# New labels and a new priority table for the scheduler of a two-layer encoder

## The chip, the cores and the metric

The kernel runs on one core of one Trainium2 chip. Its time is device microseconds (us), the median of several runs. One further execution was recorded by the profiler; its durations are used for all steps below. Engines are named as in the profile: PE is TensorE's matmul, PEld its weight load, DVE is VectorE, ACT is ScalarE, POOL is GpSimd, SP issues most of the DMAs.

## The reference

The program is an encoder of two layers on one sequence of 256 tokens with 1024 channels, in float32:

```
def reference(x, ...):
    for l in range(DEPTH):                      # DEPTH = 2
        h = hybrid_mixer(x, ...)                # three mixers on x, gated merge, w_out
        x = layer_norm(DEEPNORM_ALPHA * x + h, ln1_g[l], ln1_b[l])
        f = conv_glu_ffn(x, ffn_up[l], ffn_conv[l], ffn_conv_b[l], ffn_down[l])
        x = layer_norm(DEEPNORM_ALPHA * x + f, ln2_g[l], ln2_b[l])
    return x

def conv_glu_ffn(x, w_up, conv_w, conv_b, w_down):
    gate, up = jnp.split(x @ w_up, 2, axis=-1)  # 2 x 2816 columns
    gate = dwconv_centred(gate, conv_w) + conv_b
    return (jax.nn.silu(gate) * up) @ w_down
```

The three mixers are a differential attention, a gated DeltaNet in chunks (forward and backward, each with a triangular solve and a scan), and a windowed attention. The sum of their gated outputs goes through `w_out`.

## The kernel before

All of it runs as one stream of recorded operations on one core. Every weight matrix is cut into pieces of 128 x 1024 numbers. A piece is loaded by a DMA on SP into a `raw` tile (4 buffers), copied by ScalarE or VectorE into a `hi` tile with fewer mantissa bits, and VectorE subtracts the two to give `lo`. Each matrix product is then three products (hi x hi, lo x hi, hi x lo). There are 4 `hi` and 4 `lo` tiles; they are given out in the order in which the program asks for weights, not in the order in which TensorE uses them. In the trace the pieces are called `raw_take`, `hi_take` and `lo_take`, or `hi_proj_tok` and `lo_proj_tok` for the output projections.

The program of a layer is: three mixers in threads that ask for projections (tiles `mm_proj_ch`, `mm_token_major`), the gate and branch products of the merge (`mm_product`), the output projection `wo` with the first norm (`proj_tok`, tiles `mm_run` and `ch_run`), the feed-forward stage, and the down projection `fd` with the second norm, by the same `proj_tok`. The DeltaNet's parts show as `decay` (POOL selects and ScalarE scalings that build `D_decay` and `N_decay`), `gdn`, `solve` and `scan`.

The feed-forward stage has 22 gate and 22 up tiles of 128 columns, in 11 chunks of two (`c` = 0 to 10, the loop from line 1471). A gate or up tile is a `wide` product, `mm_wide`: eight pairs of one matmul of 512 columns with `hi` and one of 256 with `lo`. For the chunks 0 and 1 the up half comes from one product with the tokens in rows (`token_major("ft", ...)`), whose result is then transposed by TensorE; in the trace these are the eight matmuls `tile_encoder_trunk<-tri,s_token_major` (layer 1: `ile_encoder_trunk<-tri,s_token_major`). Up times activated gate gives the two operands `h_` and `l_` of a chunk on VectorE and ScalarE, also named `tile_encoder_trunk`. The down projection reads chunk 0 first.

The order of all this isn't that of the program. A class `Plan` records each operation with its engine, a modelled cost and its dependencies (`record`, whose line 195 is therefore the line of every operation in the trace). `emit` gives each operation a rank: the modelled length of the longest path that starts from it, plus the operation's urgency, plus a number from the table `PRIO` that is looked up by the operation's label:

```
op.rank += op.urgent + PRIO.get(op.label, 0.0)
```

`schedule` then simulates the engines and the tile slots, and whenever an engine is free it takes, of the operations that can start first, the one of the highest rank. The operations are issued in the order of the simulated starts. On the chip each engine works through its own list in that order, and an instruction that has to wait holds up all that stand behind it on its engine. So the table `PRIO` (numbers in us) sets the order without touching what is computed. Before, only the parts of the mixers and of the merge have labels; `proj_tok`, the norms' ends and the feed-forward stage run with label `None` and priority 0.

Of the kernel before, what the change touches and what calls it, by code (L numbers as in the profile page):

```python
# [45 lines left out]
SPOT = {('ft', 0, 0): 'g', ('ft', 0, 1): 'g', ('ft', 0, 2): 'yc', ('ft', 1, 0): 'g', ('ft', 1, 1): 'g', ('ft', 1, 2): 'yc', ('av', 1, 0): 'h16'}  # L46
DIRECT = False
WHOLE = ()
PRIO = {(0, 'a', 'ak', 0): 2.2, (0, 'a', 'ak', 1): -4.9, (0, 'a', 'aq', 1): -2.6, (0, 'a', 0): 4.1, (0, 'a', 1): -5.5, (0, 'a', 2): 1.0, (0, 'a', 3): -2.7, (0, 'ab', 0): 4.3, (0, 'ak', 0): -2.5, (0, 'aq', 0): 1.1, (0, 'aq', 1): 1.1, (0, 'av', 0): 5.7, (0, 'c', 'ckv', 0): -8.6, (0, 'c', 'cq', 0): 1.8, (0, 'c', 'cq', 1): 9.5, (0, 'c', 0): -2.0, (0, 'c', 1): -1.0, (0, 'c', 2): -4.2, (0, 'c', 3): 4.2, (0, 'ckv', 0): -4.2, (0, 'cq', 0): 1.8, (0, 'cq', 1): 11.9, (0, 'finish'): 8.4, (0, 'gate', 0): -15.6, (0, 'gate', 1): -3.2, (0, 'gz', 1): -1.6, (0, 'gz', 3): 2.0, (0, 'gz', 4): -8.6, (0, 'gz', 5): -0.8, (0, 'k', 'gate', 0): 2.5, (0, 'k', 'k', 0): -7.3, (0, 'k', 'k', 1): -0.5, (0, 'k', 'q', 0): 1.6, (0, 'k', 'q', 1): -2.1, (0, 'k', 'v', 1): 0.3, (0, 'k', 0): -3.5, (0, 'k', 1): -5.6, (0, 'q', 1): 6.9, (0, 'scan'): -13.4, (0, 'v', 0): -0.8, (0, 'wb', 0): -7.9, (0, 'wb', 1): -20.3, (0, 'wb', 2): 9.2, (0, 'wb', 3): 0.9, (0, 'wb', 4): -5.6, (1, 'a', 'ak', 0): -4.0, (1, 'a', 'ak', 1): 6.5, (1, 'a', 'aq', 0): 5.4, (1, 'a', 'aq', 1): 3.6, (1, 'a', 3): 0.3, (1, 'ab', 0): -3.6, (1, 'ak', 0): 0.4, (1, 'ak', 1): 6.6, (1, 'aq', 1): -0.3, (1, 'c', 0): 6.5, (1, 'c', 1): 0.8, (1, 'c', 3): -10.4, (1, 'ckv', 0): -4.2, (1, 'cq', 0): 7.6, (1, 'cq', 1): -10.9, (1, 'finish'): 6.3, (1, 'gate', 0): 2.0, (1, 'gate', 1): -2.8, (1, 'gz', 0): -2.9, (1, 'gz', 2): 2.1, (1, 'gz', 3): -3.6, (1, 'gz', 4): 1.2, (1, 'gz', 5): 12.7, (1, 'k', 'ab', 0): -3.9, (1, 'k', 'gate', 0): 9.3, (1, 'k', 'gate', 1): 6.1, (1, 'k', 'k', 0): 4.3, (1, 'k', 'q', 0): -5.8, (1, 'k', 'q', 1): -4.7, (1, 'k', 'v', 0): 5.9, (1, 'k', 'v', 1): -1.4, (1, 'k', 1): -5.3, (1, 'q', 0): 10.2, (1, 'q', 1): -4.3, (1, 'scan'): -5.9, (1, 'solve'): -3.9, (1, 'wb', 0): -10.8, (1, 'wb', 1): -23.6, (1, 'wb', 3): 6.8, (1, 'wb', 4): 4.9, (1, 'wb', 5): 13.3, (0, 'k', 'ab', 0): -1.4, (0, 'k', 'gate', 1): -0.1, (0, 'k', 'v', 0): 4.3, (0, 'q', 0): 0.2, (1, 'aq', 0): -3.6, (1, 'av', 0): -1.9, (1, 'gz', 1): 0.7, (1, 'v', 0): 4.6, (1, 'wb', 2): 4.1}
LOADS = (11, 12, 12)  # L50
PIECES = 2
PAIRS = ("s", "yc")
# [86 lines left out]
class Plan:  # L139
# [99 lines left out]
    def emit(self):  # L239
# [45 lines left out]
        for op in ops:  # L285
            op.rank += op.urgent + PRIO.get(op.label, 0.0)
        self.schedule(users, order)
# [208 lines left out]
def tile_encoder_trunk(ctx: ExitStack, tc: tile.TileContext, a: dict, out: bass.AP, depth=DEPTH, tap=None):  # L496
    nc = tc.nc
    plan = Plan()
# [15 lines left out]
    def nm(base):  # L514
        import sys
        f = sys._getframe(2)
        base = f"{base}_{f.f_code.co_name}{f.f_lineno}"
        counts[base] = counts.get(base, 0) + 1
        return f"{base}_{counts[base]}"
# [4 lines left out]
    def buf(tag, shape=(P, 512), dtype=F32):  # L524
        return plan.tile(mp, shape, dtype, tag, nm(tag), BUFS[tag])
# [47 lines left out]
    x = cp.tile([P, 2, D], F32, name="x")  # L573
# [256 lines left out]
    def proj_tok(nme, l, nk, lhs, norm):  # L830

        nb = nk // 2
        order = [(half, b) for half in range(2) for b in range(nb)]
        plain, tags = KEEP[nme] if nme == "wo" else KEEP[nme][l]
        first = len(order) - plain - len(tags)
        ps = {}

        def run(half, b, w, tt, c0=0):
            n = 256 if half == tt == 1 and SPLIT else 512
            if (half, tt, c0) not in ps:  # L840
                ps[half, tt, c0] = (ps_ch if half == 1 and (c0 == 0 or SPLIT == 2) else ps_mm)((P, n))
            cs = slice(c0, c0 + n)
            for j in range(2):
                k = 2 * b + j
                lh, ll = lhs(k, tt)
                mm3(ps[half, tt, c0], lh, ll, w[0][j][:, cs], w[1][j][:, cs], k == 0, k == nk - 1)
            if b == nb - 1:
                u, plan.urgent = plan.urgent, HASTE if tt and half else HASTE0
                norm.part(tt, half * 512 + c0, n, ps[half, tt, c0])
                plan.urgent = u  # L850

        kept = []
        for n, (half, b) in enumerate(order):
# [679 lines left out]
```

## Time and profile before

| | us |
|---|---|
| median of 3 runs | 986.03 (985.98 to 986.37) |
| the profiled execution, its own time | 985.31 |
| its span in the trace | 983.6 |
| PE busy | 961.5 (98%) |
| PEld busy | 829.6 (84%) |
| DVE busy | 759.4 (77%) |
| ACT busy | 605.8 (62%) |
| POOL busy | 75.1 (8%) |

Busy time is the share of the span in which an engine executes at least one instruction. Matmuls overlap in the pipeline, so a matmul's shown length is longer than the step from one to the next. The trace also gives, for each instruction that its engine had to wait for, how long the engine was idle ahead of it and which instruction released it.

### The profile page before, as it was taken

How to read it: one execution, taken by the hardware profiler on the slowest of the kernel's cores; microseconds unless marked ns; L12 is line 12 of the kernel's file. 1: busy time of each engine (PE TensorE's matmuls, PEld its weight loads, DVE VectorE, ACT ScalarE, POOL GpSimd, SP SyncE). 2: the span in 40 equal slices, each digit the busy share in tenths (PEclk: the TensorE clock that was granted, in tenths of full speed). 3: DMA queues.
4: the chain of work that ended last, by engine and by line, in shares of the span. 5: the costliest groups of instructions: out<-in, count | busy, mean ns of one | idle time of the engine just before them, and what ended most of it. 6: DMA issues, size and time to landing. Idle time of an engine off the chain costs nothing.

```text
span 983.6 us, 16368 instructions
## 1 busy us (share of the span) xinstructions
PE 961.5 (98%) x6126; PEld 829.6 (84%) x6126; DVE 759.4 (77%) x1404; ACT 605.8 (62%) x1134; POOL 75.1 (8%) x84
## 2 busy tenths in 40 slices
PE   7999999999999999999999999999999999999996
PEld 6889899878888888878889998998778778888885
DVE  6799797666599988875689989866565988888655
ACT  5778757774465766653558777756744646666441
POOL 0510020000000100000005200100000010000000
PEclk9999999999999999999999999999999999999999
DMA  7554435355685766656635444334556665666661
GB/s 266 151 170 133 126 135 187 92 157 164 192 268 164 211 193 191 192 153 192 213 92 168 159 144 131 117 107 131 174 167 200 220 193 185 179 189 191 192 192 43
DMA packets 50100, 165.27 MB, mean 168 GB/s; under 512 B 5751, under 2 KB 11271, under 8 KB 50020
## 3 DMA queue, kind: packets, MB, share of 16 engines
q1 hardware_dynamic: 48644, 159.78, 52.3%
q0 software_dynamic: 1376, 4.43, 1.5%
q8 instruction: 48, 0.79, 0.3%
q14 instruction: 32, 0.26, 0.1%
HBM read 163.12 MB, written 1.07 MB: 167 GB/s over the span
## 4 chain that ended last, share of the span: by engine, by line
PE 83%; DVE 5%; ACT 4%; DMA 3%; issue 2%; POOL 2%; SPq 0%; POOLq 0%; ACTq 0%; DVEq 0%
PE mm_wide L195 23%; PE mm_product L195 19%; PE mm_proj_ch L195 15%; PE mm_run L195 7%; PE ch_run L195 6%; PE mm_token_major L195 3%; PE at_window L195 3%; PE ch_solve L195 2%; PE at_attention L195 2%; DMA raw_take<-in_w_dram 1%; ACT hi_take L195 1%; PE ch_gdn L195 1%; PE ch_finish L195 1%; PE ch_scan L195 1%; DVE lo_take L195 1%
## 5 line engine op out<-in xcount | busy, mean ns | idle before, releaser
L195 DVE TENSOR_TENSOR lo_take<-raw_take,hi_take 128x1024 fp32r<-128x1024 f32 x219 | 269.5, 1236 | 96.1 <-ACT hi_take L195 93.3
L195 ACT ACTIVATE hi_take<-raw_take 128x1024 fp32r<-128x1024 f32 x213 | 224.3, 1057 | 178.9 <-PE mm_wide L195 59.3
L195 PE MATMUL mm_wide<-xT,hi_take 128*128 128x512 f32 x640 | 224.0, 394 | 0.1
L195 PE MATMUL mm_proj_ch<-xT,hi_take 128*128 128x256 f32 x928 | 177.8, 287 | 1.1 <-ACT hi_take L195 1.1
L195 PE MATMUL mm_wide<-xT,lo_take 128*128 128x256 f32 x640 | 178.3, 283 | 0.0
L195 PEld LDWEIGHTS mm_proj_ch<-xT,hi_take 128*128 128x128 f32 x928 | 144.7, 189 | 4.2 <-ACT hi_take L195 1.7
L195 PEld LDWEIGHTS mm_wide<-xT,hi_take 128*128 128x128 f32 x640 | 119.4, 188 | 26.6 <-DVE xT L195 0.3
L195 PE MATMUL mm_proj_ch<-xT,lo_take 128*128 128x256 f32 x464 | 133.4, 288 | 0.0
L195 PE MATMUL mm_product<-hi_take,xT 128*128 128x512 f32 x384 | 128.4, 403 | 0.0
L195 PEld LDWEIGHTS mm_wide<-xT,lo_take 128*128 128x128 f32 x640 | 120.4, 188 | 1.4
L195 DVE TENSOR_TENSOR lo_proj_tok<-raw_proj_tok,hi_proj_tok 128x1024 fp32r<-128x1024 f32 x50 | 61.2, 1224 | 46.0 <-ACT hi_proj_tok L195 45.9
L195 ACT ACTIVATE hi_proj_tok<-raw_proj_tok 128x1024 fp32r<-128x1024 f32 x50 | 53.0, 1060 | 63.8 <-PE mm_run L195 35.0
L195 PEld LDWEIGHTS mm_proj_ch<-xT,lo_take 128*128 128x128 f32 x464 | 87.6, 189 | 2.7 <-DVE lo_take L195 1.1
L195 PEld LDWEIGHTS mm_product<-hi_take,xT 128*128 128x128 f32 x384 | 71.5, 189 | 15.4 <-issue 1.5
L195 PE MATMUL mm_product<-lo_take,xT 128*128 128x512 f32 x192 | 77.2, 402 | 0.0
L195 PEld LDWEIGHTS mm_product<-lo_take,xT 128*128 128x128 f32 x192 | 36.3, 189 | 6.8 <-DVE lo_take L195 0.2
L195 DVE SCALAR_TENSOR_TENSOR z_conv_silu<-mm_proj_ch,col_params,z_conv_silu 128x254 f32<-128x254 f32 (+1 forms) x96 | 39.4, 473 | 0.2
L195 POOL TENSOR_TENSOR s_tail<-s_tail,nhalf 128x1 f32<-128x1 f32 x8 | 8.2, 1023 | 383.4 <-DVE s_tail L195 383.4
L195 ACT ACTIVATE e_window<-e_window,s_window 128x256 f32<-128x256 f32 x54 | 25.7, 499 | 12.2 <-DVE s_window L195 12.1
L195 PEld LDWEIGHTS <-h_solve 128*128 128x128 f16 x640 | 25.6, 98 | 7.8 <-issue 3.4
L195 PE MATMUL mm_run<-hi_proj_tok,tile_encoder_trunk 128*128 128x512 f32 x88 | 27.5, 392 | 2.4 <-DVE tile_encoder_trunk L195 1.4
L195 PE MATMUL mm_run<-hi_proj_tok,ile_encoder_trunk 128*128 128x512 f32 x88 | 27.3, 390 | 0.0
(354 smaller groups left out, 1771.6 us busy)
## 6 DMA issues: line engine op xcount, KB each, us to landing
raw_take<-in_w_dram SPq DMA_DIRECT2D x226, 512.0 KB, 3.7
raw_proj_tok<-in_w_dram SPq DMA_DIRECT2D x60, 512.0 KB, 3.6
G_load_G<-band SPq DMA_DIRECT2D x24, 192.0 KB, 3.3
ya_ln_params<-in_lnp_dram POOLq DMA_DIRECT2D x16, 256.0 KB, 5.4
x<-in_xT_dram SPq DMA_DIRECT2D x4, 256.0 KB, 4.3
x<-in_x_dram SPq DMA_DIRECT2D x2, 512.0 KB, 4.5
out_dram<-x SPq DMA_DIRECT2D x8, 128.0 KB, 1.7
_tile_encoder_trunk<-in_w_dram SPq DMA_DIRECT2D x4, 128.0 KB, 5.1
```

What stands on the lines that cost most here:

```text
L195: op.ways.append((eng, lambda fn=fn, args=args, kw=kw: fn(*args, **kw), _cost(eng, name, outs, ins, args, kw), table))
```

## The change

The table `PRIO` is replaced: all its numbers are new, and it has entries for new labels. These labels are set in three places: in `proj_tok` for each weight piece (layer, `fd` or `wo`, half, piece), for the norm's two tails and for the pieces that are kept for a second pass; in the layer loop around the last step of a norm (`norms.pop().finish()`); and in the feed-forward stage for the token-major product and for each chunk. No operation, operand, tile or modelled cost is changed. Cut to its core:

```diff
-PRIO = {(0, 'a', 'ak', 0): 2.2, ...}
+PRIO = {(0, 'a', 'ak', 0): -4.7, ..., (0, 'f', 5): -8.9, ..., (0, 'ft'): 1.2, ..., (1, 'f', 7): -11.7, ...}
...
         kept = []
         for n, (half, b) in enumerate(order):
+            plan.label = (l, nme, half, b)
             w = weights((nme, l, half, b), tag=tags[n - first - plain] if n >= first + plain else None)
...
+        plan.label = (l, nme, "tail", 0)
         norm.tail(0)
+        plan.label = (l, nme, "kept")
         for c0 in (0, 256) if SPLIT else (0,):
...
+        plan.label = (l, nme, "tail", 1)
         norm.tail(1)
+        plan.label = None
...
         if norms:
+            plan.label = (l, "x", 2)
             norms.pop().finish()
+            plan.label = None
...
+        plan.label = (l, "ft")
         ft = token_major("ft", l, "s")
         for c in range(NFF // 2):
+            plan.label = (l, "f", c)
             pg = buf("h16", (P, 2, T))
...
             if c == 2:
+                plan.label = (l, "x", 1)
                 norms.pop().finish()
+        plan.label = None
         norm = Norm(l, 2, pr["ln2_g"], pr["ln2_b"], l == depth - 1)
```

How the order moves is seen in the engines' lists. In layer 0 ScalarE, where the DeltaNet's decay matrices are made, has this before (`N_decay` are the scalings that wait for POOL's selects, `hi_take_9` is the copy of the ninth weight piece):

```order
L195 ACTIVATE N_decay_1_125<-N_decay_1_125,nbeta_gdn_scalars_1_109 128x128 x4
L195 ACTIVATE N_decay_2_130<-N_decay_2_130,nbeta_gdn_scalars_1_109 128x128 x3
L195 ACTIVATE hi_take_9_182<-raw_take_9_181 128x1024
L195 ACTIVATE N_decay_2_130<-N_decay_2_130,nbeta_gdn_scalars_1_109 128x128
L195 ACTIVATE N_decay_3_135<-N_decay_3_135,nbeta_gdn_scalars_1_109 128x128 x4
L195 ACTIVATE N_decay_4_140<-N_decay_4_140,nbeta_gdn_scalars_1_109 128x128 x4
```

The ninth copy stands behind seven scalings. The same engine after, from four places ahead of the first copy of `D_decay`:

```order
L195 ACTIVATE hi_take_7_169<-raw_take_7_168 128x1024
L195 ACTIVATE q_token_major_1_154<-mm_token_major_1_153 128x512
L195 ACTIVATE hi_take_8_172<-raw_take_8_171 128x1024
L195 ACTIVATE hi_take_9_182<-raw_take_9_181 128x1024
L195 ACTIVATE D_decay_1_124<-ch_decay_1_123 128x512
```

and eleven places further on, where the scalings are:

```order
L195 ACTIVATE hi_take_10_185<-raw_take_10_184 128x1024
L195 ACTIVATE N_decay_1_125<-N_decay_1_125,nbeta_gdn_scalars_1_109 128x128 x4
L195 ACTIVATE N_decay_2_130<-N_decay_2_130,nbeta_gdn_scalars_1_109 128x128 x3
L195 ACTIVATE D_decay_4_139<-ch_decay_4_138 128x512
L195 ACTIVATE N_decay_2_130<-N_decay_2_130,nbeta_gdn_scalars_1_109 128x128
L195 ACTIVATE N_decay_3_135<-N_decay_3_135,nbeta_gdn_scalars_1_109 128x128 x4
L195 ACTIVATE hi_take_11_264<-raw_take_11_263 128x1024
```

The copies 7 to 10 have moved ahead of the scalings; the eleventh is now among them.

On TensorE, at the end of layer 0's feed-forward stage, before (`mm_wide_40` is the last up tile, `mm_run_3` the first tile of the down projection, which reads chunk 0; the transposes have `mm_` ahead of the trace's name, after their PSUM tile):

```order
L195 MATMUL mm_wide_40_969<-xT,hi_take_109_971 128x512
L195 MATMUL mm_wide_40_969<-xT,lo_take_109_972 128x256
L195 MATMUL mm_tile_encoder_trunk_1_770<-tri,s_token_major_1_757 128x128
L195 MATMUL mm_tile_encoder_trunk_1_770<-tri,s_token_major_2_759 128x128
L195 MATMUL mm_tile_encoder_trunk_1_770<-tri,s_token_major_1_757 128x128
L195 MATMUL mm_tile_encoder_trunk_1_770<-tri,s_token_major_2_759 128x128
L195 MATMUL mm_tile_encoder_trunk_2_783<-tri,s_token_major_1_757 128x128
L195 MATMUL mm_tile_encoder_trunk_2_783<-tri,s_token_major_2_759 128x128
L195 MATMUL mm_tile_encoder_trunk_2_783<-tri,s_token_major_1_757 128x128
L195 MATMUL mm_tile_encoder_trunk_2_783<-tri,s_token_major_2_759 128x128
L195 MATMUL mm_run_3_984<-hi_proj_tok_6_982,z_tile_encoder_trunk_1_771 128x512
L195 MATMUL mm_run_3_984<-lo_proj_tok_6_983,z_tile_encoder_trunk_1_771 128x512
```

After, the four transposes of chunk 0 stand some 400 rows earlier, between gate tiles (`mm_wide_12` and `mm_wide_17`), and those of chunk 1 earlier still:

```order
L195 MATMUL mm_wide_12_822<-xT,lo_take_81_825 128x256
L195 MATMUL mm_tile_encoder_trunk_1_770<-tri,s_token_major_1_757 128x128
L195 MATMUL mm_tile_encoder_trunk_1_770<-tri,s_token_major_2_759 128x128
L195 MATMUL mm_tile_encoder_trunk_1_770<-tri,s_token_major_1_757 128x128
L195 MATMUL mm_tile_encoder_trunk_1_770<-tri,s_token_major_2_759 128x128
L195 MATMUL mm_wide_17_850<-xT,hi_take_86_852 128x512
```

and the down projection's first matmul comes while chunk 5's up tiles (`mm_wide_19`, `mm_wide_20`) are unfinished:

```order
L195 MATMUL mm_wide_19_860<-xT,lo_take_88_863 128x256
L195 MATMUL mm_wide_20_864<-xT,hi_take_89_866 128x512
L195 MATMUL mm_wide_20_864<-xT,lo_take_89_867 128x256
L195 MATMUL mm_wide_20_864<-xT,hi_take_89_866 128x512
L195 MATMUL mm_wide_20_864<-xT,lo_take_89_867 128x256
L195 MATMUL mm_wide_20_864<-xT,hi_take_89_866 128x512
L195 MATMUL mm_wide_20_864<-xT,lo_take_89_867 128x256
L195 MATMUL mm_wide_20_864<-xT,hi_take_89_866 128x512
L195 MATMUL mm_wide_20_864<-xT,lo_take_89_867 128x256
L195 MATMUL mm_run_3_984<-hi_proj_tok_6_982,z_tile_encoder_trunk_1_771 128x512
```

The other matmuls of `mm_wide_19` stand 200 to 300 rows earlier; 18 other wide tiles (`mm_wide_21` to `mm_wide_38`) lie between. In layer 1 chunk 7's up tiles are treated alike, with 12 wide tiles between.

## Rows read from the trace of the kernel before

**Rows 1.** The page: busy time of each engine, its share of the span, instructions.

```profile
PE 961.5 (98%) x6126; PEld 829.6 (84%) x6126; DVE 759.4 (77%) x1404; ACT 605.8 (62%) x1134; POOL 75.1 (8%) x84
```

**Rows 2.** Timeline, TensorE's last matmuls: start, busy us, engine, line, operation.

```profile
973.68 0.84 PE L195 MATMUL ch_run<-g_weights,ile_encoder_trunk 128*128 128x512 f32 x3
```

**Rows 3.** Waits of TensorE, whole span: total us, times, longest us.

```profile
PE mm_proj_ch L195 <- ACT _tile_encoder_trunk L195: 5.9, 2, 4.9
PE mm_run L195 <- DVE tile_encoder_trunk L195: 1.4, 1, 1.4
PE mm_proj_ch L195 <- ACT hi_take L195: 1.1, 2, 0.8
PE mm_run L195 <- ACT tile_encoder_trunk L195: 1.0, 1, 1.0
PE ile_encoder_trunk L195 <- ACT s_token_major L195: 0.7, 1, 0.7
PE ch_solve L195 <- DVE h_solve L195: 0.7, 1, 0.7
PE mm_token_major L195 <- DVE xT L195: 0.6, 1, 0.6
PE ch_solve L195 <- ACT h_solve L195: 0.6, 2, 0.4
PE at_window L195 <- DVE s_window L195: 0.3, 1, 0.3
PE ch_gdn L195 <- ACT j_gdn L195: 0.3, 1, 0.3
PE at_window L195 <- DVE o_attention L195: 0.2, 1, 0.2
```

**Rows 4.** Timeline, end of layer 0's feed-forward stage; idle before and releaser in brackets.

```profile
428.20 0.39 PE L195 MATMUL mm_wide<-xT,hi_take 128*128 128x512 f32 x1
428.43 0.28 PE L195 MATMUL mm_wide<-xT,lo_take 128*128 128x256 f32 x1
...
428.55 0.40 PE L195 MATMUL mm_wide<-xT,hi_take 128*128 128x512 f32 x1
...
429.60 1.04 PE L195 MATMUL tile_encoder_trunk<-tri,s_token_major 128*128 128x128 f32 x8
...
431.64 0.50 PE L195 MATMUL mm_run<-hi_proj_tok,tile_encoder_trunk 128*128 128x512 f32 x1 [1.01 <-ACT tile_encoder_trunk L195]
...
432.31 3.08 DVE L195 TENSOR_TENSOR tile_encoder_trunk<-tile_encoder_trunk,tile_encoder_trunk 128x512 f32<-128x512 f32 x5
...
434.25 0.73 PE L195 MATMUL mm_run<-hi_proj_tok,tile_encoder_trunk 128*128 128x512 f32 x2 [1.41 <-DVE tile_encoder_trunk L195]
```

**Rows 5.** Timeline, layer 0's decay matrices, VectorE, POOL, ScalarE and TensorE.

```profile
34.61 3.22 DVE L195 TENSOR_TENSOR lo_take<-raw_take,hi_take 128x1024 fp32r<-128x1024 f32 x2
...
36.70 1.61 POOL L195 TENSOR_SCALAR_AFFINE_SELECT N_decay<-D_decay 128x512 f32<-128x512 f32 x1
...
38.35 2.16 ACT L195 ACTIVATE N_decay<-N_decay,nbeta_gdn_scalars 128x128 f32<-128x128 f32 x7 [2.33 <-POOL N_decay L195]
...
40.42 1.04 ACT L195 ACTIVATE hi_take<-raw_take 128x1024 fp32r<-128x1024 f32 x1
...
41.52 0.63 PE L195 MATMUL mm_proj_ch<-xT,hi_take 128*128 128x256 f32 x3 [0.80 <-ACT hi_take L195]
```

**Rows 6.** Timeline, the first solve of layer 0, and the transposes of layer 1.

```profile
72.07 0.62 PE L195 MATMUL ch_solve<-id,h_solve 128*128 128x128 f16 x8 [0.66 <-DVE h_solve L195]
...
806.51 0.60 ACT L195 ACTIVATE s_token_major<-mm_token_major 128x512 f32<-128x512 f32 x1 [0.42 <-PE mm_token_major L195]
...
807.16 0.33 PE L195 MATMUL ile_encoder_trunk<-tri,s_token_major 128*128 128x128 f32 x1 [0.69 <-ACT s_token_major L195]
```

**Rows 7.** Timeline, two weight slots of four in use, layer 0's feed-forward stage.

```profile
377.41 1.23 DVE L195 TENSOR_TENSOR lo_take<-raw_take,hi_take 128x1024 fp32r<-128x1024 f32 x1 [0.64 <-ACT hi_take L195]
...
379.51 0.28 PE L195 MATMUL mm_wide<-xT,lo_take 128*128 128x256 f32 x1
```

More of the change, by code (lines that the diff above doesn't have):

```diff
@@ L48 @@
 WHOLE = ()
-PRIO = {(0, 'a', 'ak', 0): 2.2, (0, 'a', 'ak', 1): -4.9, (0, 'a', 'aq', 1): -2.6, (0, 'a', 0): 4.1, (0, 'a', 1): -5.5, (0, 'a', 2): 1.0, (0, 'a', 3): -2.7, (0, 'ab', 0): 4.3, (0, 'ak', 0): -2.5, (0, 'aq', 0): 1.1, (0, 'aq', 1): 1.1, (0, 'av', 0): 5.7, (0, 'c', 'ckv', 0): -8.6, (0, 'c', 'cq', 0): 1.8, (0, 'c', 'cq', 1): 9.5, (0, 'c', 0): -2.0, (0, 'c', 1): -1.0, (0, 'c', 2): -4.2, (0, 'c', 3): 4.2, (0, 'ckv', 0): -4.2, (0, 'cq', 0): 1.8, (0, 'cq', 1): 11.9, (0, 'finish'): 8.4, (0, 'gate', 0): -15.6, (0, 'gate', 1): -3.2, (0, 'gz', 1): -1.6, (0, 'gz', 3): 2.0, (0, 'gz', 4): -8.6, (0, 'gz', 5): -0.8, (0, 'k', 'gate', 0): 2.5, (0, 'k', 'k', 0): -7.3, (0, 'k', 'k', 1): -0.5, (0, 'k', 'q', 0): 1.6, (0, 'k', 'q', 1): -2.1, (0, 'k', 'v', 1): 0.3, (0, 'k', 0): -3.5, (0, 'k', 1): -5.6, (0, 'q', 1): 6.9, (0, 'scan'): -13.4, (0, 'v', 0): -0.8, (0, 'wb', 0): -7.9, (0, 'wb', 1): -20.3, (0, 'wb', 2): 9.2, (0, 'wb', 3): 0.9, (0, 'wb', 4): -5.6, (1, 'a', 'ak', 0): -4.0, (1, 'a', 'ak', 1): 6.5, (1, 'a', 'aq', 0): 5.4, (1, 'a', 'aq', 1): 3.6, (1, 'a', 3): 0.3, (1, 'ab', 0): -3.6, (1, 'ak', 0): 0.4, (1, 'ak', 1): 6.6, (1, 'aq', 1): -0.3, (1, 'c', 0): 6.5, (1, 'c', 1): 0.8, (1, 'c', 3): -10.4, (1, 'ckv', 0): -4.2, (1, 'cq', 0): 7.6, (1, 'cq', 1): -10.9, (1, 'finish'): 6.3, (1, 'gate', 0): 2.0, (1, 'gate', 1): -2.8, (1, 'gz', 0): -2.9, (1, 'gz', 2): 2.1, (1, 'gz', 3): -3.6, (1, 'gz', 4): 1.2, (1, 'gz', 5): 12.7, (1, 'k', 'ab', 0): -3.9, (1, 'k', 'gate', 0): 9.3, (1, 'k', 'gate', 1): 6.1, (1, 'k', 'k', 0): 4.3, (1, 'k', 'q', 0): -5.8, (1, 'k', 'q', 1): -4.7, (1, 'k', 'v', 0): 5.9, (1, 'k', 'v', 1): -1.4, (1, 'k', 1): -5.3, (1, 'q', 0): 10.2, (1, 'q', 1): -4.3, (1, 'scan'): -5.9, (1, 'solve'): -3.9, (1, 'wb', 0): -10.8, (1, 'wb', 1): -23.6, (1, 'wb', 3): 6.8, (1, 'wb', 4): 4.9, (1, 'wb', 5): 13.3, (0, 'k', 'ab', 0): -1.4, (0, 'k', 'gate', 1): -0.1, (0, 'k', 'v', 0): 4.3, (0, 'q', 0): 0.2, (1, 'aq', 0): -3.6, (1, 'av', 0): -1.9, (1, 'gz', 1): 0.7, (1, 'v', 0): 4.6, (1, 'wb', 2): 4.1}
@@ new lines @@
+PRIO = {(0, 'a', 'ak', 0): -4.7, (0, 'a', 'ak', 1): 1.8, (0, 'a', 'aq', 0): 6.1, (0, 'a', 'aq', 1): -0.8, (0, 'a', 0): -1.4, (0, 'a', 1): 6.3, (0, 'a', 2): -1.5, (0, 'a', 3): 1.3, (0, 'ab', 0): 7.6, (0, 'ak', 0): 14.2, (0, 'ak', 1): -1.3, (0, 'aq', 0): -7.9, (0, 'aq', 1): -0.2, (0, 'c', 'ckv', 0): -3.6, (0, 'c', 'cq', 0): 19.0, (0, 'c', 'cq', 1): -5.3, (0, 'c', 0): -3.3, (0, 'c', 1): -5.7, (0, 'c', 2): 2.4, (0, 'c', 3): -1.4, (0, 'ckv', 0): -2.5, (0, 'cq', 0): -5.8, (0, 'cq', 1): -2.3, (0, 'f', 0): -2.3, (0, 'f', 1): 5.2, (0, 'f', 10): -9.4, (0, 'f', 2): 5.5, (0, 'f', 3): -2.9, (0, 'f', 4): 3.7, (0, 'f', 5): -8.9, (0, 'f', 6): 1.6, (0, 'f', 7): 7.3, (0, 'f', 8): 4.1, (0, 'f', 9): -0.2, (0, 'fd', 'kept'): -12.8, (0, 'fd', 'tail', 0): -7.6, (0, 'fd', 'tail', 1): 3.4, (0, 'fd', 0, 0): 0.5, (0, 'fd', 0, 1): 10.8, (0, 'fd', 0, 10): 0.8, (0, 'fd', 0, 2): 3.2, (0, 'fd', 0, 3): 5.8, (0, 'fd', 0, 4): -6.2, (0, 'fd', 0, 5): -4.4, (0, 'fd', 0, 6): 0.7, (0, 'fd', 0, 7): 5.1, (0, 'fd', 0, 9): 9.1, (0, 'fd', 1, 0): -1.5, (0, 'fd', 1, 2): -6.7, (0, 'fd', 1, 4): -3.2, (0, 'fd', 1, 5): -1.8, (0, 'fd', 1, 6): 1.3, (0, 'fd', 1, 7): -1.9, (0, 'fd', 1, 8): 5.3, (0, 'fd', 1, 9): -3.5, (0, 'finish'): -1.3, (0, 'ft'): 1.2, (0, 'gate', 0): -0.9, (0, 'gate', 1): -4.4, (0, 'gz', 1): -2.0, (0, 'gz', 2): -3.5, (0, 'gz', 3): -3.9, (0, 'gz', 4): -7.2, (0, 'k', 'gate', 0): -1.6, (0, 'k', 'gate', 1): -0.3, (0, 'k', 'k', 0): 8.7, (0, 'k', 'q', 0): -0.7, (0, 'k', 'q', 1): -0.4, (0, 'k', 'v', 0): 3.9, (0, 'k', 'v', 1): -0.9, (0, 'k', 0): 1.3, (0, 'k', 1): 3.1, (0, 'q', 1): 2.0, (0, 'scan'): -2.1, (0, 'solve'): -8.0, (0, 'v', 0): -0.7, (0, 'v', 1): 1.8, (0, 'wb', 0): 0.6, (0, 'wb', 1): -72.7, (0, 'wb', 2): 8.2, (0, 'wb', 3): 5.9, (0, 'wb', 4): -1.2, (0, 'wo', 'kept'): -4.8, (0, 'wo', 'tail', 0): 0.8, (0, 'wo', 'tail', 1): 1.4, (0, 'wo', 0, 0): 0.4, (0, 'wo', 0, 1): -4.3, (0, 'wo', 0, 2): 1.8, (0, 'wo', 0, 3): 6.9, (0, 'wo', 1, 1): 4.5, (0, 'wo', 1, 2): -4.8, (0, 'wo', 1, 3): 2.6, (0, 'x', 1): 6.4, (1, 'a', 'ak', 0): 7.4, (1, 'a', 'ak', 1): 6.3, (1, 'a', 'aq', 0): 2.5, (1, 'a', 'aq', 1): -2.2, (1, 'a', 0): 0.7, (1, 'a', 1): 10.6, (1, 'a', 2): 6.5, (1, 'a', 3): 1.4, (1, 'ab', 0): -8.4, (1, 'ak', 0): -4.9, (1, 'ak', 1): 1.0, (1, 'aq', 0): 5.9, (1, 'aq', 1): 11.2, (1, 'av', 0): 2.3, (1, 'c', 'ckv', 0): -12.3, (1, 'c', 'cq', 1): 3.7, (1, 'c', 2): -0.1, (1, 'c', 3): -15.5, (1, 'ckv', 0): 6.7, (1, 'cq', 1): -7.8, (1, 'f', 1): 1.3, (1, 'f', 10): -3.2, (1, 'f', 2): 2.1, (1, 'f', 3): 5.0, (1, 'f', 5): -6.0, (1, 'f', 6): -5.7, (1, 'f', 7): -11.7, (1, 'f', 8): -1.7, (1, 'f', 9): 18.2, (1, 'fd', 'kept'): -8.0, (1, 'fd', 'tail', 0): -5.5, (1, 'fd', 0, 0): -1.1, (1, 'fd', 0, 1): 4.4, (1, 'fd', 0, 10): -1.5, (1, 'fd', 0, 2): -0.1, (1, 'fd', 0, 4): -9.0, (1, 'fd', 0, 5): 4.1, (1, 'fd', 0, 6): 2.9, (1, 'fd', 0, 7): 8.4, (1, 'fd', 0, 8): -0.6, (1, 'fd', 0, 9): -2.1, (1, 'fd', 1, 0): -4.7, (1, 'fd', 1, 1): 8.1, (1, 'fd', 1, 10): 3.2, (1, 'fd', 1, 3): 7.5, (1, 'fd', 1, 5): -5.5, (1, 'fd', 1, 6): -4.6, (1, 'fd', 1, 9): -0.8, (1, 'finish'): 6.7, (1, 'gate', 0): 4.9, (1, 'gate', 1): -2.0, (1, 'gz', 2): 2.5, (1, 'gz', 4): -1.9, (1, 'gz', 5): -15.4, (1, 'k', 'k', 0): -2.5, (1, 'k', 'k', 1): 0.1, (1, 'k', 'q', 0): -0.9, (1, 'k', 'q', 1): -2.4, (1, 'k', 'v', 0): -5.5, (1, 'k', 'v', 1): -4.4, (1, 'k', 1): 3.8, (1, 'q', 0): -2.9, (1, 'q', 1): 31.0, (1, 'scan'): -1.6, (1, 'solve'): 3.6, (1, 'v', 0): 12.4, (1, 'v', 1): 4.1, (1, 'wb', 1): 2.3, (1, 'wb', 2): 6.8, (1, 'wb', 4): 15.9, (1, 'wb', 5): -1.3, (1, 'wo', 'kept'): -8.1, (1, 'wo', 'tail', 0): -9.2, (1, 'wo', 'tail', 1): -1.0, (1, 'wo', 0, 0): -3.7, (1, 'wo', 0, 1): 9.0, (1, 'wo', 0, 3): -0.4, (1, 'wo', 1, 0): -0.9, (1, 'wo', 1, 1): -1.5, (1, 'wo', 1, 2): -0.7, (1, 'x', 1): 6.3, (1, 'x', 2): -6.7}
```

## The prediction

> **What bounds the kernel now.** I read the busy line of the page first, then the waits of TensorE, then the stretches around its longest waits, and last the weights' copies in the feed-forward stage. The busy line gives TensorE 961.5 of 983.6 us, VectorE 759.4, ScalarE 605.8 [rows 1]. TensorE's last matmul is over at 973.68 + 0.84 = 974.52 [rows 2]; the 9.1 us behind it are the last norm's chain. Of the 22.1 us that TensorE is idle, 9.1 lie there, and 12.8 are listed by cause: 5.9 before and just after its first matmul, at start-up, and 6.9 in the middle of the program [rows 3]. So nothing but TensorE's own list sets the time between 5 and 974 us, and a new order can win only what it wastes there.
>
> How much one wait wastes is read at the biggest place. A wide matmul is shown as 0.39 long, but the next one starts 0.23 after it [rows 4]: they overlap by 0.16. After a wait there is no overlap, so each wait costs its shown idle and about 0.16 more; the first matmul after it may take longer too (0.50 instead of 0.39 at 431.64 [rows 4]: 0.11).
>
> The Trainium skill ("Perfetto Trace Analysis", section Identifying the Most-Contended Engine) says that matmul busy time is a poor measure of the distance to the limit, and that weight-load busy time is a better one. By that the page's 84% [rows 1] would leave far more than 22 us to be won. The step of 0.23 in [rows 4] is what decides here: between waits the matmuls already follow at the pitch that they have in the whole stretch, and a change that adds or takes away no matmul can't shorten that pitch.
>
> **The change, part by part.** No operation is added or taken away on TensorE (6,595 instructions in either order). The labels alone do nothing; the table moves work. I name the places where TensorE waits before and ask whether the new order still has the wait.
>
> *Place D, the end of the feed-forward stage of layer 0.* Before, the eight transposes of `ft` (chunks 0 and 1) are the last thing before the down projection, which begins with just these chunks. So behind the transposes at 429.60 the path goes through VectorE and ScalarE and back: 1.01 idle at 431.64, and 1.41 at 434.25 behind five VectorE operations of 3.08 together [rows 4]. After, the transposes stand among the gate tiles hundreds of matmuls earlier, chunks 0 and 1 are long done, and the first down matmuls are set between tiles of chunk 5. What is late next is the first down weight (it takes the slot that chunk 5's first up tile gives back), behind 14 wide matmuls; those are 7 x (0.23 + 0.12) = 2.5 us by the steps of [rows 4], against one low copy of 1.23 [rows 7]. I take both waits as gone: 2.42 + 2 x 0.16 + 0.11 = 2.85. Ends: 1.41 of it comes back through the down weights (saving 1.3), or all goes (2.9).
>
> *Place A, 41.5 us.* ScalarE's copy of weight 9 starts at 40.42, behind seven `N_decay` scalings that began at 38.35 after a wait on POOL; TensorE waits 0.80 for it [rows 5]. After, copies 7, 8 and 9 stand ahead of the first `D_decay`, and copy 10 ahead of the first scaling; only copy 11 is still among them, and its first matmul stands some 70 proj matmuls of 0.12 (8 us) behind the row where its slot comes free. Saving 0.80 + 0.16 = 0.96.
> A cost stands against it. VectorE's low copies took 1.61 each (3.22 for two) beside POOL's select, which itself took 1.61 [rows 5]; elsewhere a low copy takes 1.23 [rows 7]. After, two more low copies stand between the `x_decay` products. The Trainium skill ("SBUF — State Buffer", section Who interferes with whom) has a rule for that: a VectorE operation with two SBUF inputs and a GpSimd operation that reads SBUF lock each other out, the later one blocked entirely. Read as a full block of each of the two, it would put POOL's selects 2 x 1.23 later, and where the 8 us ahead of copy 11 didn't cover that, A would save nothing: a sum of 4.0 and 982.0. The rows bear out that the two hinder each other, not a full block: by them each pair costs VectorE 1.61 - 1.23 = 0.38, and the cover holds. Ends for A: a saving of 0.96, or a new wait of the same size, 0.
>
> *Place B, the first solve (72.07, 0.66 from VectorE), and place C, a later solve step of layer 0 (0.4 from ScalarE)* [rows 3, 6]. Before B, the new order puts about 26 proj matmuls at 0.12 and 12 product matmuls at 0.23, 5.9 us, where there were some 23 of 0.12, 2.8 us; VectorE has its score reductions ahead of that chain now, which makes the chain about as long as the cover, so B may come back in part. At C whole proj blocks of 48 matmuls (5.7 us) now lie between solve steps. Savings: B 0.82, C 0.4 + 0.16 = 0.55; ends 0 and 1.4.
>
> *Place E, layer 1's first transposes (807.16, 0.69 from ScalarE)* [rows 6]. They stood directly behind the token-major matmuls whose copy they read. After, six or more token-major matmuls of the other half and five wide ones stand between: at least 1.3 us against a copy of 0.60 [rows 6] with its hand-offs. Saving 0.69 + 0.16 = 0.85; ends 0 and 0.85.
>
> *What stays.* The other waits of [rows 3]: the norm's 0.6 before token-major matmuls, 0.3 of the proj matmuls, a rest of 0.2 in the solves, 0.3, 0.3 and 0.2 in window and gdn; the start; and the tail, whose order on every engine is the same. Two ScalarE table loads around layer 0's feed-forward stage go, on an engine 62% busy, beside wide matmuls: nothing.
>
> *What is added: two weights held longer.* Four high and four low weight slots rotate in program order. After, layer 0's two up tiles of chunk 5 and layer 1's two of chunk 7 keep low slots while 18 and 12 other wide tiles run. Before shows such a stretch of two slots at 377: the low copy ends 377.41 + 1.23 = 378.64, its first use is at 379.51, 0.87 later, without a wait [rows 7]. A VectorE operation that cuts in takes some 0.62 (3.08 for five [rows 4]); one fits. I charge 1.0 us for all new waits in the program: two of the small kind of [rows 3] (0.3 with 0.16 more) make 0.9, rounded up. Ends: 0 (the 0.87 holds everywhere), and 30 x 0.24 = 7.2 (rival 2).
>
> **Sum.** 2.85 + 0.96 + 0.82 + 0.55 + 0.85 = 6.0 saved, 1.0 lost: 5.0 against the profiled execution's 985.31, so 980.3. The median of the runs is 986.03, 0.72 above that execution; with it 981.0.
>
> **Rivals.**
> 1. *The waits only move.* The solves and norms are chains across engines; a filler used early is missing later, and C's neighbours and the norm may take back what A, B, C and E gave (3.2). For it: B's chain is as long as its cover; layer 1's first proj tile keeps its weights while others pass. Against it: D is 2.85 by itself and nothing of that chain is left near the end. It gives 2.85 - 1.0 - 0.9 (one more wait like E's): 985.1.
> 2. *Slower: two slots starve the feed-forward stage.* With two low slots, high copy 1.04 [rows 5], low copy 1.23 and two hand-offs must fit beside one wide tile of 16 matmuls, 8 x 0.35 = 2.8 us; only 0.87 is left over [rows 7]. Two VectorE operations of 0.62 that stand between exceed it by 0.4. If most of the 30 tiles come 0.24 late, 7.2 are lost instead of 1.0: 986.03 - 6.0 + 7.2 = 987.2, and with the 0.11 that a restart costs at each of them 990.5. It is slower than now by 2 us from a mean lateness of 0.27 per tile. Against it: the order was laid out so that low copies stand ahead of the convolution work in the rows I read, and 377 shows no wait.
> 3. *More than forecast.* All 6.9 us of middle idle go, with 13 overlaps of 0.16, 2.1: 9.0, so 977.0; the small lateness at change-overs may add a little. For it: the solves get long fillers in both layers. Against it: the norm before the token-major matmuls keeps its order.
>
> **How the numbers follow.** About 2 us (0.2%) is what a measurement here can tell from no change. The forecast (977.5 to 983.5 on its own) gets 0.60. Rival 1 gets 0.17: 0.11 within 0.2%, 0.04 faster, 0.02 slower. Rival 2 gets 0.13, of which 0.12 slower and 0.01 within. Rival 3 gets 0.10. So faster 0.74, same 0.12, slower 0.14. The range reaches from 975.0 (a little beyond rival 3) to 987.0 (rival 1 and the mild edge of rival 2).
>
> **What would show it.** In the profile of the changed kernel, TensorE's waits should sum to some 9 us instead of 12.8, with no wait of the down matmuls on `tile_encoder_trunk`, none of the layer 1 transposes on `s_token_major`, and the busy time of TensorE unchanged within a few us. The last matmul should end near 969.5, with the same 9.1 us behind it. Wrong if wide tiles list waits on low or high copies in the feed-forward stage (rival 2), or if D's 2.4 us turn up again at the down weights.

## The result and the profile after

The changed kernel takes 980.23 us (median of 4 runs, 978.58 to 981.76) against 986.2 (four runs); the ratio is 0.9944, with an interval of 0.9931 to 0.9957. The forecast was 981.0, 5.0 less than before by the terms of its sum. Run again in another job it took 978.82 against 986.25: 0.992 (0.9904 to 0.9935). So the gain is 6.0 us in the first job and 7.4 in the second, a little more than forecast.

The page's busy line of the profiled execution (978.58 us, span 976.9):

```profile
PE 956.3 (98%) x6126; PEld 826.7 (85%) x6126; DVE 762.8 (78%) x1409; ACT 602.7 (62%) x1127; POOL 74.3 (8%) x84
```

TensorE is idle for 976.9 - 956.3 = 20.6 us, only 1.5 less than before [rows 1]. Its busy time fell by 5.2, which I had said would stay within a few us. Its last matmuls, to be held against [rows 2]:

```profile
966.74 1.07 PE L195 MATMUL ch_run<-g_weights,ile_encoder_trunk 128*128 128x512 f32 x4
```

They are over at 967.81, 6.7 earlier than 974.52; the 9.1 us behind them stayed. The waits of TensorE, as in [rows 3] (total us, times, longest):

```profile
PE mm_proj_ch L195 <- ACT _tile_encoder_trunk L195: 5.2, 2, 4.9
PE ch_decay L195 <- DVE x_decay L195: 1.1, 3, 0.7
PE mm_run L195 <- ACT kk_product L195: 0.7, 1, 0.7
PE at_window L195 <- DVE e_window L195: 0.6, 1, 0.6
PE mm_proj_ch L195 <- ACT hi_take L195: 0.6, 1, 0.6
PE mm_token_major L195 <- DVE xT L195: 0.5, 1, 0.5
PE mm_product L195 <- DVE lo_take L195: 0.5, 1, 0.5
PE ch_gdn L195 <- DVE z_conv_silu L195: 0.3, 1, 0.3
...
PE ch_solve L195 <- ACT h_solve L195: 0.2, 1, 0.2
```

The rows of the five places are gone: no down matmul waits on `tile_encoder_trunk`, no transpose on `s_token_major`, and of the solves 0.2 is left; the row on `hi_take` is now a tile of layer 1 at 537. Others have come: `x_decay`, `e_window`, a low copy ahead of a product, the convolution. With the rows left out here they sum to 11.0 in all where I expected some 9.

Two traces of each order tell apart what belongs to the order and what to the execution (the second ones are from the runs `e11_before_again` and `e1_again` below). What a wait costs is the time from start to start of the two matmuls around it, less its usual step:

| place | before, two traces | after, two traces |
|---|---|---|
| A, proj, layer 0 | 0.96, 0.95 | gone |
| B, first solve | 0.82, 0.83 | gone |
| C, solve step | 0.56, 0.57 | gone |
| D, transposes to down projection | 2.74, 2.75 | gone |
| E, transposes of layer 1 | 0.86, 0.86 | gone |
| a window step, layer 0 | 0.57, 0.62 | 0.78, 0.89 |
| decay, gdn, product, layer 0 | none | 0.86 + 0.52 + 0.69, 0.86 + 0.52 + 0.70 |
| window value matmuls, all steps | 11.90, 11.90 | 9.79, 9.82 |
| first 48 matmuls, all steps | 10.57, 8.85 | 8.65, 10.03 |

All rows but the last repeat to about 0.1 and so belong to the order. The last row is start-up, which swings by 1.7 us in the old order and by 1.4 in the new one and is no effect of the change.

The five places cost 5.9 before. The table names only some of the waits that came instead. Counted in the same way, all other listed waits of the middle that stand in both traces of an order cost 2.9 before and 6.6 to 6.7 after; besides those of the table it is mainly layer 1's decay products, 0.38 + 0.32. So the new waits take back 3.7.

### The profile page after: what moved, and what is told of

It is laid out like the page before. It is cut to its first block, busy times and chain, and to the rows that moved or that the text cites. A ratio compares the mean times of both kernels' runs of the same rounds, so it can differ in the third digit from the quotient of the medians.

```text
span 976.9 us, 16398 instructions
## 1 busy us (share of the span) xinstructions
PE 956.3 (98%) x6126; PEld 826.7 (85%) x6126; DVE 762.8 (78%) x1409; ACT 602.7 (62%) x1127; POOL 74.3 (8%) x84
## 5 line engine op out<-in xcount | busy, mean ns | idle before, releaser
L195 ACT ACTIVATE hi_take<-raw_take 128x1024 fp32r<-128x1024 f32 x211 | 221.7, 1057 | 144.2 <-PE mm_product L195 50.9
L195 DVE SCALAR_TENSOR_TENSOR z_conv_silu<-mm_proj_ch,col_params,z_conv_silu 128x255 f32<-128x255 f32 (+1 forms) x96 | 39.9, 472 | 1.5 <-ACT z_conv_silu L195 1.3
```

The lines of the kernel that those rows point to most:

```text
L195: op.ways.append((eng, lambda fn=fn, args=args, kw=kw: fn(*args, **kw), _cost(eng, name, outs, ins, args, kw), table))
```

## The experiments

Each stands beside runs of the kernel before on its own chip; the medians of before were 986.25 (for `e1` to `e4`), 985.11 (`e5` to `e8`), 986.1 (`e9` to `e11`) and 985.29 (`e12`).

**The changed kernel and the old order once more.** `e1_again` has no edit; `e11_before_again` has the new labels and the old table.

> The changed kernel once more, unaltered, for a second trace and a better median. Theory: 980.2, within 978.5 to 982; the waits of 0.5 us and more stand at the same places (the decay products near 32, gdn near 54, a window step and a product near 200, token-major near 490, a proj tile near 536, the output projection of layer 1 near 761), so they come from the order. Rival (chance of the run): some of these waits are gone and others of 0.5 us and more appear, and the start-up, 1.9 us shorter than before in the first trace, is back to that of before.

> The old table once more, for a second trace of the old order. Theory: the places A to E have the same waits within 0.1 us (0.8, 0.7, 0.4, 1.0 and 1.4, 0.7), and start-up differs by up to 1 us. Rival (some of the five places were chance): one of them is missing.

978.82 and 987.09 (one run). Except for one of 0.86 in layer 1's output projection, the waits of 0.5 and more of the first trace of the changed kernel are at their places; all five places of the old order are back to 0.1, so the labels by themselves cure none of them. Start-up aside, two larger things differ between the two traces of the old order. One is a wait in the tail of layer 0's first norm, at 300, which costs 1.37 in steps and which the first trace doesn't list:

```profile
PE ch_tail L195 <- DVE q_tail L195: 1.2, 1, 1.2
```

It belongs to the execution and not to the order: the two traces of the changed kernel have 0.3 and nothing there, and that of `e7_fours_new` has 1.0. The other is the granted clock behind D. Windows of 5 us in the first trace of the old order (length, busy time and instructions of PE, PEld, DVE, ACT, POOL, then the granted clock as a share of full speed, DMA share, GB/s):

```profile
430.00:435.00 5.00, 2.58 (x13) 1.74 (x12) 4.89 (x9) 2.82 (x5) 0.00 (x0) 1.00 0.67 209
435.00:440.00 5.00, 5.00 (x23) 4.10 (x23) 1.62 (x2) 1.88 (x2) 0.00 (x0) 1.00 0.04 11
```

and in its second trace:

```profile
430.00:435.00 5.00, 2.59 (x13) 1.73 (x12) 4.89 (x9) 2.88 (x5) 0.00 (x0) 0.88 0.60 205
435.00:440.00 5.00, 5.00 (x19) 4.00 (x18) 1.56 (x2) 1.06 (x1) 0.00 (x0) 0.78 0.01 5
```

The same two waits; in one execution TensorE keeps its upper level of 2.4 GHz, in the other it falls to the lower one for a while. Its timeline behind the second wait:

```profile
434.30 1.22 PE L195 MATMUL mm_run<-hi_proj_tok,tile_encoder_trunk 128*128 128x512 f32 x2 [1.41 <-DVE tile_encoder_trunk L195]
435.32 0.63 PE L195 MATMUL mm_run<-lo_proj_tok,tile_encoder_trunk 128*128 128x512 f32 x1
...
438.07 0.62 PE L195 MATMUL mm_run<-hi_proj_tok,tile_encoder_trunk 128*128 128x512 f32 x2
```

From 434.30 to 438.07 ten matmuls are started, in 3.77 us; in the first trace the ten behind the same wait took 2.42, so 1.3 is lost. D cost 2.7 in the one execution and some 4.1 in the other.

**D alone.** Two entries are added to the old table:

```diff
-PRIO = {(0, 'a', 'ak', 0): 2.2, ...}
+PRIO = {(0, 'a', 'ak', 0): 2.2, ..., (0, 'f', 0): 2, (0, 'f', 1): 2}
```

> The old table with two entries of 2.0 for the chunks 0 and 1 of layer 0's feed-forward stage and nothing else: the eight transposes stand some 500 rows earlier, all other engines but for a few dozen rows as before. Theory (D is worth 2.85 and nothing of it comes back): 983.3, from 982.7 to 984.2; the waits of the down matmuls of 1.41 and 1.01 are gone from the trace, perhaps a wait of 0.7 on the token-major copy appears, as E's. Rival (the waits only move): 985.2 or more, with a new wait at the down weights.

982.19 against 986.25, ratio 0.995 (0.9933 to 0.9967): 4.1 us, more than half of the whole gain from two numbers, and a little more than the forecast range gave. The waits of its trace:

```profile
PE mm_proj_ch L195 <- ACT _tile_encoder_trunk L195: 5.5, 2, 5.1
PE mm_proj_ch L195 <- ACT hi_take L195: 0.8, 1, 0.8
PE ile_encoder_trunk L195 <- ACT s_token_major L195: 0.7, 1, 0.7
PE ch_solve L195 <- DVE h_solve L195: 0.6, 1, 0.6
PE ch_solve L195 <- ACT h_solve L195: 0.6, 2, 0.4
```

Both waits of the down matmuls are gone and those of A, B, C and E are as before. That the gain is above 2.85 agrees with the clock, which fell behind D in one trace of the old order and had nothing to fall behind here. How often it falls there, and so whether this is the whole excess, is not shown.

**D put back into the new order.**

```diff
-(0, 'f', 0): -2.3, (0, 'f', 1): 5.2
+(0, 'f', 0): -10, (0, 'f', 1): -10
```

> The changed kernel with the chunks 0 and 1 of layer 0 at -10.0 instead of -2.3 and 5.2, so that the eight transposes are again the last thing before the down projection; nearly all else keeps its place. Theory (D is the largest part of the gain, also within the new order): the two waits of 1.0 and 1.4 us are back in the trace, and the time is 2.85 to 4.0 above that of the changed kernel (978.8 to 980.2): 982 to 984. Rival (with the new order the down weights or other tiles cover the transposes): within 1 us of it.

987.2 against 985.11: 1.0014 (1.0004 to 1.0025). The whole gain is lost, more than either theory gave. The trace tells why (waits, then windows):

```profile
PE mm_wide L195 <- ACT hi_take L195: 1.6, 1, 1.6
PE mm_run L195 <- DVE tile_encoder_trunk L195: 1.6, 1, 1.6
PE mm_run L195 <- ACT tile_encoder_trunk L195: 1.5, 1, 1.5
```

```profile
430.00:435.00 5.00, 2.23 (x7) 1.52 (x8) 5.00 (x9) 2.30 (x5) 0.00 (x0) 0.91 0.58 202
435.00:440.00 5.00, 5.00 (x18) 3.99 (x17) 0.11 (x1) 0.00 (x0) 0.00 (x0) 0.75 0.00 1
```

D's waits came back larger (3.1 instead of 2.4), the clock fell behind them, and the two numbers also moved a weight copy near 320, which adds 1.6 of idle. So this run shows that D is as costly in the new order, but not its size alone.

**Each half of the table by itself.** One kernel keeps only those entries of the new table whose labels existed before; the other has the old table and the entries of the new labels (written short here; in the kernels the tables are spelled out):

```diff
+PRIO = {k: v for k, v in PRIO.items() if k[1] not in ('f', 'ft', 'fd', 'wo', 'x')}    # e2_mixers_only
+PRIO = {**OLD, **{k: v for k, v in PRIO.items() if k[1] in ('f', 'ft', 'fd', 'wo', 'x')}}    # e3_stage_only
```

> The new table without its entries for the new labels (feed-forward chunks, ft, output projections, norms). Theory (gains sit at places): A, B and C go (0.96 + 0.82 + 0.55 = 2.3), D stays (the eight transposes of layer 0 are last again), and in layer 1 the transposes are last too, so a wait like D's 2.4 us of idle appears there instead of E's 0.69: 986.2 - 2.3 + 2.0 + 0.5 for small new ones = 986.4, from 985 to 988. Rival (the mixers' new numbers bring the whole gain): 980 to 982.

> The old numbers for the mixers, with the new entries for the new labels. Theory: D and E go (2.85 + 0.85 = 3.7), A, B and C stay as before, up to 1.5 of new small waits in layer 1, whose order moves too: 983.0, from 982 to 985. Rival (the gain needs both halves of the table, since the order of layer 1 follows from both): 985 or more.

990.96 (987.09 to 994.4) and 990.61: ratios 1.0041 and 1.0039, both intervals above 1.002. Neither half gains; the first forecast missed by 4.6, the second by 7.6, and of the two rivals that of the second holds: the gain needs both halves. Waits of the first, and a window:

```profile
PE mm_proj_ch L195 <- DVE lo_take L195: 1.9, 1, 1.9
PE mm_run L195 <- DVE ile_encoder_trunk L195: 1.4, 1, 1.4
PE mm_run L195 <- DVE tile_encoder_trunk L195: 1.4, 1, 1.4
```

```profile
525.00:530.00 5.00, 4.53 (x25) 4.53 (x26) 5.00 (x4) 4.29 (x12) 5.00 (x4) 0.66 0.60 172
```

A, B and C are gone and D is there in both layers, as expected. The new waits of the changed kernel in layer 0's mixers are there too, so they come from these numbers. A low copy in layer 1 comes 1.9 late, with the clock at 0.66 behind it. The fastest run, the profiled one at 987.09, has a mean clock of 0.996; the slowest, 994.4, has 0.992. That the slower runs lose the clock at more of these places would fit; no trace of one shows it. The second half alone:

```profile
PE mm_token_major L195 <- DVE xT L195: 2.4, 3, 1.5
PE mm_product L195 <- ACT N_decay L195: 1.8, 1, 1.8
PE at_window L195 <- DVE s_window L195: 1.5, 2, 1.2
```

```profile
540.00:545.00 5.00, 4.82 (x16) 3.79 (x17) 4.80 (x9) 4.96 (x10) 0.00 (x0) 0.66 0.34 102
```

D and E are gone there too and A, B and C stand, but layer 1's mixers, with their old numbers behind a feed-forward stage that ends in another order, have new long waits. The two halves of the table fit each other, not the other's old half.

**The held weights.** In the first kernel the entries `(0, 'f', 5)` and `(1, 'f', 7)` are taken out of the new table; in the second the old table gets the one entry `(0, 'f', 5): -8.9`.

> The changed kernel without the priorities of chunk 5 in layer 0 and chunk 7 in layer 1, whose up tiles then run in turn instead of holding two of the four weight slots past 18 and 12 other tiles. Theory (the held slots cost nothing: no wide tile waits in the trace): within 1 us of the changed kernel, 978 to 981. Rival (two slots make the wide tiles late by pieces too small to be listed): 1 to 3 us faster, 976 to 978.

> The old table with one new entry, chunk 5 of layer 0 at -8.9 as in the new table. Its up tiles then come last, one of them between the first matmuls of the down projection, and the scheduler puts the eight transposes some 400 rows earlier by itself. Theory (D goes either way, 2.85 by the trace and about 4 by the medians, as in the run that moved the transposes alone): 3 to 4.5 us less than before, and no wait of the down matmuls on tile_encoder_trunk. Rival (the held weights starve the tiles in between, or the down projection then waits for its own weights): at most 1.5 us less.

984.87 against 985.11 (0.9999, 0.9991 to 1.0008), and 989.61 against 986.1 (1.0035). Both theories fall, and the first one's rival too: without the held tiles the new order is some 6 us slower, not faster. The second is slower than the old order, on the side that its rival named, but not for the rival's reasons. The waits of the first kernel are

```profile
PE mm_run L195 <- ACT ile_encoder_trunk L195: 1.7, 1, 1.7
PE mm_wide L195 <- DVE lo_take L195: 1.1, 2, 0.7
```

As I read the trace, the tiles that are put off are work that TensorE has at hand when the last chunk's operands are still being made: without them it waits for those operands in layer 1's down projection, behind the last wide tile, and loses 1.8 in steps. Two low copies come late in the wide tiles, 1.4 together, for which I have no reason. In layer 0 the transposes of chunk 0 slip towards the end again. So the run shows that the two numbers are worth some 6 us in the new table; it doesn't try the held tiles as filler by themselves. Put off too far, as in the second kernel, the tile itself becomes what is waited for (timeline row, then a window):

```profile
449.09 0.79 PE L195 MATMUL mm_run<-hi_proj_tok,tile_encoder_trunk 128*128 128x512 f32 x1 [4.01 <-ACT tile_encoder_trunk L195]
```

```profile
450.00:455.00 5.00, 5.00 (x13) 3.92 (x13) 0.00 (x0) 0.34 (x1) 0.00 (x0) 0.51 0.07 28
```

One of chunk 5's up tiles runs between the down matmuls of the pieces 4 and 5, and piece 5 needs its product at once.

**The window's value matmuls.** The four of a head pair are issued one behind the other, at the place of the last; in the first kernel with the old table, in the second with the new one:

```diff
...
+        for four in self.four.values():
+            end = max(op.start for op in four)
+            for n, op in enumerate(sorted(four, key=lambda o: o.start)):
+                op.start = end - (3 - n) * 1e-6
         for op in sorted(ops, key=lambda o: o.start):
...
```

> The old table; the four value matmuls of each window head pair are issued one behind the other (each at the place of the last of the four), as nearly everywhere in the new order; before, five of the eight fours are split in 3 and 1. Theory (a four together takes 1.22 us, a split one 1.01 + 0.58 = 1.59, since halves of the array work side by side): 5 x 0.37 = 1.85 less than before, 984.4, from 983.8 to 985.0; the value matmuls' steps sum to 9.8 instead of 11.9 us. Rival (what is saved in them is lost in the fillers around): 985.8 to 986.6.

> The changed kernel with the one four that its order still splits put together too. Theory: 0.37 less than the changed kernel, 978.4 to 979.8, hard to tell apart in one job. Rival (no effect): the same as the changed kernel, 978.8 to 980.2.

984.84 against 985.11 (0.999, 0.998 to 1.0001) and 978.6 (0.9933, 0.992 to 0.9945). The steps of these matmuls fell as expected, from 11.90 to 9.62 in the old order, but the median fell by 0.3 only. The interval reaches from no gain to 2.0, so the rival is the likelier, and the theory's 1.85 is not excluded. A row of the old order with them put together shows the fillers missing at another place:

```profile
182.91 0.39 PE L196 MATMUL mm_proj_ch<-xT,lo_take 128*128 128x256 f32 x1 [0.72 <-DVE lo_take L196]
```

In this trace the last matmul is where it was before, at 974.5. But 0.8 of what the fours gave is lost there at the `ch_tail` of 300, which differs from execution to execution, and so how much of the 2.1 of the table above is a gain stays open. The second kernel can't be told from the changed one, as was said ahead of it.

**Place A's price.** The four `x_decay` products of POOL in layer 0 go to VectorE; the last kernel has this and the edit of the fours:

```diff
-        for eng, gs in ((G, sc["gh"]), (V, sc["gl"])):
+        for eng, gs in ((V if plan.label[0] == 0 else G, sc["gh"]), (V, sc["gl"])):
```

> The changed kernel with layer 0's four x_decay products of POOL moved to VectorE (same numbers), so that the two engines don't work side by side there. In the traces of the changed kernel the first decay matmul waits 0.7 for x_decay, 1.1 in all, while three POOL products take 1.46 each and three on VectorE 1.32. Theory (place A's gain is taken back there by the two engines hindering each other): the waits of ch_decay on x_decay go, a product takes some 0.7, and the time is 0.8 to 1.2 less than the changed kernel, 977.5 to 978.5. Rival (VectorE has no room for four more products): the same or slower, with waits on low copies between 30 and 45 us.

> The changed kernel with both edits: layer 0's four x_decay products of POOL on VectorE, and the four value matmuls of each window head pair together. Theory (the decay waits are gone and nothing takes their place): 0.9 to 1.5 us less than the changed kernel in its best jobs (978.6 and 978.8), 977.2 to 978.0, ratio to before 0.991. Rival (the median of 981.3 of the run with the decay edit alone was no chance of its job: the new order of the stretch behind it costs what is gained): 979.5 to 982, ratio 0.994 to 0.996.

981.29 against 986.1 (0.9952, 0.9934 to 0.997; 977.88 to 982.94) and 979.21 against 985.29 (0.9934, 0.9919 to 0.9948). In the changed kernel (timeline):

```profile
29.64 4.39 POOL L195 TENSOR_TENSOR x_decay<-tri,gh_gdn_scalars 128x512 fp32r<-128x512 f32 x3 [27.00 <-DVE gh_gdn_scalars L195]
...
30.60 1.01 DVE L195 TENSOR_TENSOR gl_gdn_scalars<-gg_gdn_scalars,gh_gdn_scalars 128x16 fp32r<-128x16 f32 x1
...
31.65 3.97 DVE L195 TENSOR_TENSOR x_decay<-tri,gl_gdn_scalars 128x512 fp32r<-128x512 f32 x3
...
33.18 0.50 PE L195 MATMUL ch_decay<-x_decay,strict 128*128 128x512 f32 x1 [0.69 <-DVE x_decay L195]
```

and with the products on VectorE alone:

```profile
29.81 0.18 DVE L195 TENSOR_TENSOR gl_gdn_scalars<-gg_gdn_scalars,gh_gdn_scalars 128x16 fp32r<-128x16 f32 x1
...
30.50 0.68 DVE L195 TENSOR_TENSOR x_decay<-tri,gl_gdn_scalars 128x512 fp32r<-128x512 f32 x1
```

A product takes 0.68 instead of 1.32, and the waits on `x_decay` fall from 1.1 to 0.4; what is left is layer 1's, where POOL still has its share:

```profile
PE ch_decay L195 <- DVE x_decay L195: 0.4, 2, 0.3
```

So layer 0's wait is there because the two engines work side by side. But that alone doesn't make it: in the old order they did so too, with products as slow on VectorE (before, two of 1.5 each),

```profile
28.69 2.97 DVE L195 TENSOR_TENSOR x_decay<-tri,gl_gdn_scalars 128x512 fp32r<-128x512 f32 x2
```

and TensorE lists no wait for them. The new order puts them where TensorE needs them sooner.

The time isn't better than the changed kernel's by what can be measured, and both forecasts were missed: the traces, each of the fastest execution of its job, end earliest of all (spans 976.2 and 975.9), the medians don't follow. Why the runs of the first of them spread over 5 us at a clock of 0.996 to 0.998 is open. No version here beats the changed kernel.

## Why the prediction was right, and where it was not

- *That TensorE's list alone sets the time*: right. The end moved with the last matmul, and the tail stayed 9.1.
- *D, 2.85*: right in mechanism and in size by the trace (2.74), shown by the run that moves the transposes alone. By the medians it is worth 4.1 (3.3 to 6.6). The fall of the clock behind these waits, 1.3 in one of two traces, fits the excess; that it is all of it isn't shown. I read one execution, in which the clock did not fall, and left it out.
- *A, 0.96*: the wait is gone, and nearly all of it is given back, the end that I had put at 0. I looked for the cost of POOL and VectorE side by side at copy 11, where 8 us do cover it; TensorE waits at `ch_decay`, for VectorE's own product, 0.86 in steps. The run with the products moved shows that the wait needs the two engines side by side; since the old order had them so without a wait, it needs the new order too. The Trainium skill's rule on the shared SBUF port, which I had weighed ("SBUF — State Buffer", section Who interferes with whom), fits: a VectorE operation of 16 columns took 1.01 beside POOL and 0.18 without.
- *B 0.82, C 0.55, E 0.85*: gone, as read from the order, by sizes of 0.82, 0.56 and 0.86. None was tried by itself; that they are as before in the run that moves D alone shows that it is not the transposes that cure them.
- *1.0 for all new waits*: mis-sized. Those that repeat in both traces cost 3.7, of which 0.86 + 0.52 + 0.69 are in layer 0's mixers and 0.7 at layer 1's decay products. The reason given for them, the held weights, is the step that failed: no wide tile of the changed kernel waits for its weights (the steps of all wide matmuls sum to 225.0 us, 224.9 before), and the entries that hold them are among what makes the new order fast. Rival 2 had their sign wrong.
- *Busy time of TensorE unchanged*: wrong, by 5.2. Waits shorter than a matmul's shown length, a split four of value matmuls, slower steps at start-up all count as busy. The listed idle in the middle fell from 6.9 to 5.8 only, and would by itself have said that the change does little. And a change of order alone can shorten the pitch, which I had ruled out: the steps of the window's value matmuls fell from 11.9 to 9.8.
- So the 5.0 came out near the measured 6.0 to 7.4 in part by luck, because errors oppose each other: 2.7 more of new waits than were charged, against shorter steps of the value matmuls, the clock behind D and steps too small for a list, none of which was in the sum. The last matmul ends 6.7 earlier in the first traces, of which start-up, chance, is up to 1.9.

## What to carry to other kernels

Where one engine sets the time, list its waits and ask of each what the new order puts ahead of it; then ask what is now late, above all where two engines that hinder each other get work at the same time. A tile that is put off can be filler for a junction between stages, up to the point at which its own result is needed. And a table of priorities is one piece: either half of this one with the old other half was slower than the old table.

## What the runs showed of the hardware

The granted clock fell behind some waits of TensorE and not behind others, with the same kernel and waits of the same length: behind D at 430 in the second trace of the old order (0.78 over 435 to 440), not in the first (1.00); behind single waits of 1.9 and 1.8 (0.66 over 5 us); behind the one of 4.0 (0.51); not behind one of 1.7 at 927, in the kernel without held weights:

```profile
925.00:930.00 5.00, 3.19 (x14) 1.99 (x13) 2.83 (x4) 1.58 (x2) 0.00 (x0) 1.00 0.70 218
```

So D cost its idle time in one execution and 1.3 us on top in the other.

Matmuls that use half of the array's columns run side by side when they follow each other; pairs of them start 7 ns apart in the trace. Four of the window's value matmuls together, eight records, and the same four in two pieces (before, the last two records):

```profile
197.54 1.08 PE L195 MATMUL at_window<-aT_window,sv_window 128*64 128x256 f32 x8
```

```profile
181.81 1.08 PE L195 MATMUL at_window<-aT_window,sv_window 128*64 128x256 f32 x6
...
192.48 0.65 PE L195 MATMUL at_window<-aT_window,sv_window 128*64 128x256 f32 x2
```

The eight take as long as the six, and the two left over 0.65 more.
